# Hybrid decoder layer: small weights laid out by the host, the q block's split pinned behind hT, and the gates' series moved from GpSimd to VectorE

## The chip, the core and the metric

One core of a Trainium2 chip runs the whole layer in one launch. The metric is the device time in microseconds (us) of one execution. The engines are TensorE (PE: matmuls; PEld: its weight loads), VectorE (DVE), ScalarE (ACT), GpSimd (POOL) and SyncE (SP, which issues most DMAs here). Each engine takes its instructions in the order of the program; engines wait for each other by semaphores.

## The reference

The input x has 512 tokens of 1024 channels, all float32. What matters here:

```python
h = rmsnorm(x, norm_mix_g)
proj = h @ w_in
bg, cg, xv, q, k, v, z, a, b, ga, gb = split(proj)
y_a = short_conv_branch(bg, cg, xv, conv_a_w) @ w_a_out
# the gated-DeltaNet branch, 8 heads of 128, chunks of 64
q, k, v = silu(causal_dwconv([q, k, v], gdn_conv_w))   # 4 taps, then l2norm of q and k
beta = sigmoid(b)
g = -exp(A_log) * softplus(a + dt_bias)                # the gates: 512 tokens x 8 heads
G = cumsum(g) in each chunk                            # decays exp(G_i - G_j)
...
x = x + (sigmoid(ga) * y_a + sigmoid(gb) * y_b) @ w_o
x = x + conv_ffn(rmsnorm(x, norm_ffn_g))
out = rmsnorm(x, norm_final_g)
```

softplus(u) is computed as max(u, 0) + log(1 + t) with t = exp(-|u|), and the logarithm by a series: with s = t / (t + 2), log(1 + t) = 2 s (1 + s^2/3 + s^4/5 + ... + s^14/15).

## The kernel before

Matmuls run on pairs of rounded parts: every operand is split into a high part (a cast on ScalarE, `wh` or `hT[0]`) and a rest (a subtraction on VectorE, `wl` or `hT[1]`), and a product is three matmuls. A `Block` is 1 MB of a weight (256 output columns) that is loaded into one of two `raw` buffers and split in four quarters by `part` (L137). `run_jobs` (L204) goes through a list of jobs, one block each: the k block first, then q, v, z of the first pair of heads, and so on. While a job's products are issued, `mm` (L107) counts columns, and at every slab (`SLAB` = 4 matmuls of 512 columns) `tick` (L95) advances the generators in the queues by one step: the next block's split, the evacuations (`qkv` with `conv`, L334: ScalarE scales the product from PSUM to `cv`, VectorE adds the other taps), and the chains. So the number of `yield`s in a chain says how many slabs of matmuls stand in front of its next part in the program. The compiler's scheduler then orders each engine's instructions; `keep_in_program_order` pins single ones, and inside `manual_schedule` the named engines keep the written order.

The start (L427 to L575): SP loads x in four tiles, the small weights and the k block in quarters (`load_k`). `norm_x`, `scale_x` and `turn_x` normalize a tile of x (ScalarE's square sums, VectorE, a power on GpSimd), scale it into `xr` and transpose it on TensorE (L496) into PSUM. `out_hi` (ScalarE, L499) and `out_lo` (VectorE, L503) write the two parts of hT, first for tokens 0 to 255 and then for 256 to 511, times the norm's weight, which lies in `wA`. `round_k` (L507) and `rest_k` (L511) split the k block's quarters. `k_tile` and `ab_tile` are the products of hT with the k block and with the 16 columns of a and b. `wA` holds the conv weights and the norm's, one per partition; they are loaded as rows of 128 (`wr`) and transposed on TensorE (L532), as are `wr2` and `wr3` for `wF` (L573, L574). Three matmuls on zeros (L470, `WARM`) come ahead of all.

The gates (`gates_chain`, L603): the product `abT` of a and b is transposed (L609), `abv` is its sum of parts, `u` is a + dt_bias, `t` = exp(-|u|). The series runs on GpSimd from L624 to L640 and ends in `g`. After `Y_G` = 16 more slabs two matmuls, L644 and L645, form the sums of g in a chunk and over it; G and what follows from it (`negG`, `kdv`, `eG`, `Dm` by way of a DMA) feed the chunks' triangular systems in `front`.

Of the kernel before, what the change touches and what calls it, by code (L numbers as in the profile page):

```python
# [9 lines left out]
F32 = mybir.dt.float32  # L10
F32R = mybir.dt.float32r
AF = mybir.ActivationFunctionType
ALU = mybir.AluOpType
# [3 lines left out]
P = 128  # L17
# [11 lines left out]
Y_V, Y_T, Y_G, Y_N, Y_E, SLAB = 4, 17, 16, 3, 4, 4  # L29
# [31 lines left out]
def layer_kernel(ctx, tc, x, norm_mix_g, w_in, w_ab, conv_a_w, gdn_conv_w, gdn_A_log, gdn_dt_bias,  # L61
                 gdn_norm_g, w_a_out, w_b_out, w_o, norm_ffn_g, w_up, ffn_conv_w, w_down,
# [17 lines left out]
    def bank():  # L80
        return ps.tile([P, 512], F32, tag="ps", name=nm("ps"))
# [43 lines left out]
    class Block:  # L125
        def __init__(self, src, quarter=(4, P)):
            self.src, self.quarter = src, quarter
            self.raw, self.ready, self.lead, self.fed = None, False, 2, True
            self.wh, self.wl = {}, {}
# [7 lines left out]
        def part(self, name, src):  # L137
            wh = self.wh[name] = wp.tile([P, *self.quarter], F32R, tag="wh", bufs=WQ, name=nm("wh"))
            wl = self.wl[name] = wp.tile([P, *self.quarter], F32R, tag="wl", bufs=WQ, name=nm("wl"))
            act.copy(out=wh, in_=src)  # L140
            dve.tensor_tensor(out=wl, in0=src, in1=wh.bitcast(F32), op=ALU.subtract)  # L141
# [206 lines left out]
    pool.memset(phalf, 0.5)  # L348
    wA = const.tile([P, P], F32, name="wA")
    wF = const.tile([P, 133], F32, name="wF")  # L350
# [27 lines left out]
    def load_k(q):  # L378
        nc.sync.dma_start(out=k_block.raw[:, q], in_=w_in[C_K][:, 4 * q:4 * q + 4])
# [47 lines left out]
    with tc.tile_pool(name="st1", bufs=1) as st1:  # L427
# [29 lines left out]
        dtb = gs.tile([P, H], F32, name="dtb")  # L457
        nc.sync.dma_start(out=dtb, in_=gdn_dt_bias[0].partition_broadcast(P))
        alg = gs.tile([P, H], F32, name="alg")
        nc.sync.dma_start(out=alg, in_=gdn_A_log[0].partition_broadcast(P))  # L460
        fr = ffn_conv_w.rearrange("o j (c p) -> (o j c) p", p=P)
        wr2 = st1.tile([66, P], F32, name="wr2")
        nc.sync.dma_start(out=wr2, in_=fr[0:66])
        wr3 = st1.tile([67, P], F32, name="wr3")
        nc.sync.dma_start(out=wr3[0:66], in_=fr[66:132])
        nc.sync.dma_start(out=wr3[66:67], in_=gdn_norm_g)

        po = bank()
        for _ in range(WARM):
            pe.matmul(po[:, 0:512], lhsT=warm[:, 0:P], rhs=warm[:, 0:512], start=True, stop=True)  # L470
        po = bank()
# [21 lines left out]
        def turn_x(t, bs):  # L493
            for k in range(ND):
                c = (k % 2) * HS + (t % 2) * P
                pe.transpose(out=bs[k // 2][:, c:c + P], in_=xrs[t][:, k * P:(k + 1) * P], identity=ident)  # L496
# [31 lines left out]
        with tc.manual_schedule(engines={mybir.EngineType.DVE, mybir.EngineType.Activation, mybir.EngineType.Pool}):  # L528
# [12 lines left out]
            o_ab, o_k = bank(), [bank(), bank()]  # L541
            for ks in (lower, upper):
                for k in ks:
                    out_hi(0, bs, k)
                for k in ks:
                    out_lo(0, bs, k)
                    k_tile(0, k)
                    ab_tile(k)
                if ks is lower:
                    rest_k(1)  # L550
# [21 lines left out]
        po = bank()  # L572
        pe.transpose(out=po[:, 0:66], in_=wr2, identity=ident[:66, :66])  # L573
        pe.transpose(out=po[:, 66:133], in_=wr3, identity=ident[:67, :67])  # L574
        dve.tensor_copy(out=wF, in_=po[:, 0:133])  # L575
# [8 lines left out]
    def hn(ap):  # L584
        return ap.rearrange("p (h n) -> p h n", n=NT)
# [17 lines left out]
    def gates_chain(o):  # L603
# [20 lines left out]
        pool.tensor_scalar(z, t, 2.0, None, op0=ALU.add)  # L624
        yield
        dve.reciprocal(out=beta, in_=beta)
        dve.reciprocal(out=z, in_=z)
        dve.tensor_scalar(u, u, 0.0, None, op0=ALU.max)
# [7 lines left out]
        pool.tensor_tensor(out=q, in0=q, in1=t, op=ALU.mult)  # L636
        pool.tensor_scalar(q, q, 2.0, None, op0=ALU.mult)
        pool.tensor_tensor(out=g, in0=q, in1=u, op=ALU.add)
        pool.tensor_tensor(out=hn(g), in0=hn(g), in1=alg.unsqueeze(2).broadcast_to([P, H, NT]), op=ALU.mult)
        pool.tensor_scalar(g, g, -1.0, None, op0=ALU.mult)  # L640
# [357 lines left out]
    jobs.insert(14, jobs.pop(11))  # L998

# [599 lines left out]
    def down_place(i):  # L1599
# [19 lines left out]
_INS = ['x', 'norm_mix_g', 'w_in', 'w_ab', 'conv_a_w', 'gdn_conv_w', 'gdn_A_log', 'gdn_dt_bias', 'gdn_norm_g',  # L1619
        'w_a_out', 'w_b_out', 'w_o', 'norm_ffn_g', 'w_up', 'ffn_conv_w', 'w_down', 'norm_final_g']  # L1620
# [3 lines left out]
def laid_out(inputs):  # L1624

# [13 lines left out]
    a["w_ab"] = np.ascontiguousarray(w[:, 7168:7184].reshape(ND, P, 16).transpose(1, 0, 2))  # L1639
# [29 lines left out]
```

## Time and profile before

| | |
|---|---|
| median of 3 runs | 966.83 us (965.64 to 966.93) |
| the profiled execution | 966.41 us, span 964.7 us |
| TensorE, VectorE, ScalarE, GpSimd busy | 99%, 77%, 52%, 16% of the span |
| mean granted TensorE clock | 0.996 |
| TensorE busy in 0 to 5, 5 to 10, 10 to 15 us | 3.48, 3.30, 3.51 us |
| TensorE busy in 15 to 20, 20 to 25, 25 to 30 us | 5.00, 4.94, 5.00 us |
| VectorE busy in 30 to 40 us | 9.63 us |

A row of the timeline gives the start in us from the span's start, the duration, the engine, the line of the program, the operation, what it writes and reads, and in brackets how long the engine was idle before it and what ended that. A duration may overlap the next instruction's start, since the engines work in pipelines; so what an instruction costs its queue is the distance from its start to the next one's. A row of waits names the engine and line that waited, what ended the wait, the total in us, how many times, and the longest.

### The profile page before, as it was taken

The page shows a single profiled execution, that of the slowest core. Times are in us where ns is not written, and L with a number is a line of the kernel's source. Part 1 is how long each engine was busy: PE and PEld are TensorE (multiplying, and loading weights), DVE is VectorE, ACT ScalarE, POOL GpSimd, SP SyncE. Part 2 cuts the span into 40 slices and gives each one's busy share as a digit, 9 for nine tenths or more (in the row PEclk, how much of TensorE's full clock was granted, in tenths as well). Part 3 has the DMA queues.
Part 4 walks back from the last instruction along what each step waited for, and adds up shares of the span by engine and source line. Part 5 has one row for each costly group of instructions (what it writes and reads, how often), then busy time and mean ns, then how long its engine had stood idle before and what let it go on. Part 6 is the DMA issues. An engine that isn't in the chain of part 4 may idle for free.

```text
span 964.7 us, 16169 instructions
## 1 busy us (share of the span) xinstructions
PE 951.5 (99%) x6178; PEld 822.6 (85%) x6178; DVE 743.1 (77%) x1401; ACT 505.9 (52%) x1073; POOL 157.1 (16%) x251
## 2 busy tenths in 40 slices
PE   8999999999999999999999999999999999999996
PEld 6888887887878889999988888998889999888885
DVE  5968686796735957799863479999988888969775
ACT  6795656566444424444751235645645456546463
POOL 3330300202000202312232100223222210000000
PEclk9999999999999999999999999999999999999999
DMA  6443422213121456756878436594774783176332
GB/s 227 155 139 95 121 53 89 74 47 103 53 88 45 133 130 138 200 147 160 232 256 173 124 104 225 149 232 154 174 189 177 193 163 131 45 260 230 99 131 87
DMA packets 51630, 138.11 MB, mean 143 GB/s; under 512 B 21692, under 2 KB 22113, under 8 KB 42849
## 3 DMA queue, kind: packets, MB, share of 16 engines
q1 hardware_dynamic: 38864, 107.45, 32.5%
q0 software_dynamic: 12544, 29.37, 16.3%
q8 instruction: 48, 0.79, 0.3%
q14 instruction: 30, 0.24, 0.1%
q10 hardware_dynamic: 144, 0.26, 0.1%
HBM read 133.64 MB, written 32.78 MB: 173 GB/s over the span
## 4 chain that ended last, share of the span: by engine, by line
PE 91%; DVE 4%; ACT 1%; issue 1%; POOL 1%; POOLq 0%
PE ps L108 83%; PE ps L681 1%; PE ps L716 1%; DVE wl L141 1%; PE ps L890 1%; PE ps L910 1%; DVE h L1327 1%; PE ps L899 0%; DVE hn L1313 0%; PE ps L878 0%; PE ps L877 0%; PE ps L854 0%; PE ps L848 0%; POOL r L1311 0%; PE ps L792 0%
## 5 line engine op out<-in xcount | busy, mean ns | idle before, releaser
L108 PE MATMUL ps<-hT,wh 128*128 128x512 f32 (+1 forms) x1104 | 319.1, 368 | 1.6 <-ACT hT L499 1.5
L140 ACT CAST wh<-raw 128x512 fp32r<-128x512 f32 x350 | 203.0, 618 | 220.8 <-PE ps L108 142.5
L141 DVE TENSOR_TENSOR wl<-raw,wh 128x512 fp32r<-128x512 f32 x350 | 232.3, 689 | 58.5 <-ACT wh L140 57.5
L108 PEld LDWEIGHTS ps<-hT,wh 128*128 128x128 f32 x1104 | 197.4, 190 | 30.6 <-ACT hT L499 1.7
L108 PE MATMUL ps<-hT,wl 128*128 128x512 f32 (+1 forms) x552 | 195.4, 362 | 0.0
L108 PE MATMUL ps<-h,wh 128*128 128x512 f32 (+1 forms) x704 | 177.7, 341 | 0.4 <-DVE h L1327 0.4
L108 PEld LDWEIGHTS ps<-h,wh 128*128 128x128 f32 x704 | 122.3, 189 | 15.7 <-DVE h L1327 0.6
L108 PEld LDWEIGHTS ps<-hT,wl 128*128 128x128 f32 x552 | 104.6, 190 | 13.8
L108 PE MATMUL ps<-h,wl 128*128 128x512 f32 (+1 forms) x352 | 114.5, 341 | 0.0
L108 PE MATMUL ps<-wh,xs 128*128 128x512 f32 (+1 forms) x320 | 96.9, 384 | 0.0
L108 PEld LDWEIGHTS ps<-h,wl 128*128 128x128 f32 x352 | 66.6, 189 | 7.6
L108 PEld LDWEIGHTS ps<-wh,xs 128*128 128x128 f32 x320 | 59.6, 188 | 13.1
L223 POOL COPY gate<-raw 1x1 f32<-1x1 f32 x38 | 19.7, 518 | 272.9 <-DMA raw<-in_w_in_dram 119.7
L108 PE MATMUL ps<-wl,xs 128*128 128x512 f32 (+1 forms) x160 | 62.1, 388 | 0.0
L108 PE MATMUL ps<-ts,wh 128*128 128x256 f32 x320 | 56.2, 276 | 0.0
L338 DVE SCALAR_TENSOR_TENSOR cv<-ps,wA,cv 128x511 f32<-128x511 f32 (+2 forms) x72 | 53.2, 741 | 3.9 <-ACT cv L335 3.7
L140 ACT CAST wh<-raws 128x512 fp32r<-128x512 f32 x66 | 39.2, 618 | 26.9 <-PE ps L108 8.6
L141 DVE TENSOR_TENSOR wl<-raws,wh 128x512 fp32r<-128x512 f32 x66 | 42.9, 687 | 12.6 <-ACT wh L140 12.5
L161 DVE TENSOR_TENSOR raw<-raw 128x512 f32<-128x512 f32 x72 | 49.4, 686 | 1.4
L108 PEld LDWEIGHTS ps<-ts,wh 128*128 128x128 f32 x320 | 49.0, 188 | 0.0
L108 PE MATMUL ps<-us,wh 128*128 128x256 f32 x256 | 45.0, 276 | 0.0
L108 PE MATMUL ps<-yas,wh 128*128 128x512 f32 x128 | 40.3, 394 | 0.0
(316 smaller groups left out, 1546.2 us busy)
## 6 DMA issues: line engine op xcount, KB each, us to landing
raw<-in_w_in_dram SPq DMA_DIRECT2D x35, 1024.0 KB, 4.9
raw<-in_w_up_dram SPq DMA_DIRECT2D x22, 1024.0 KB, 5.0
dv<-in_w_down_dram POOLq DMA_DIRECT2D x50, 256.0 KB, 6.2
raws<-dv SPq DMA_DIRECT2D x8, 768.0 KB, 7.2
ov<-in_w_o_dram POOLq DMA_DIRECT2D x20, 256.0 KB, 5.1
raws<-in_w_down_dram SPq DMA_DIRECT2D x10, 512.0 KB, 5.0
raw<-in_w_a_out_dram SPq DMA_DIRECT2D x4, 1024.0 KB, 5.9
raw<-in_w_b_out_dram SPq DMA_DIRECT2D x4, 1024.0 KB, 8.0
```

What stands on the lines that cost most here:

```text
L108: pe.matmul(o, lhsT=a, rhs=b, start=start, stop=stop, skip_group_check=free)
L140: act.copy(out=wh, in_=src)
L141: dve.tensor_tensor(out=wl, in0=src, in1=wh.bitcast(F32), op=ALU.subtract)
L161: dve.tensor_tensor(out=r[q], in0=a, in1=b, op=op)
L223: tc.keep_in_program_order(pool.tensor_copy(out=gate[:, 0:1], in_=el[:, 0:1]))
L338: dve.scalar_tensor_tensor(out=dst[:, sh:], in0=src[:, :S - sh], scalar=wcol(j), in1=dst[:, sh:], op0=ALU.mult, op1=ALU.add)
L681: pe.transpose(out=o[:, n * P:(n + 1) * P], in_=src[:, n * P:(n + 1) * P], identity=ident)
L716: pe.matmul(o[:, i], lhsT=kqs[:, a, h, 0, sl], rhs=kqs[:, b, h, :, sl], start=a > 0, stop=a + b == 0)
L890: pe.matmul(o[:, 0:P], lhsT=TTf[:, f, :], rhs=rs[h], start=True, stop=True)
L910: pe.matmul(o[:, 0:P], lhsT=A[:, f, :], rhs=vns[h], start=True, stop=True)
L1327: dve.tensor_tensor(out=h2[1][:, 4 * g:4 * g + 4, t * P:(t + 1) * P], in0=ov, in1=hs.bitcast(F32), op=ALU.subtract)
```

## The change

- The host lays out the small weights: `small_mix` (what `wA` holds) and `small_rest` (what `wF` holds, with A_log and dt_bias repeated over the partitions) come by one DMA each, already with one value per partition. The transposes and copies from `wr`, `wr2` and `wr3` are gone. SP issues the first quarter of the k block ahead of the small weights.
- TensorE gets five matmuls of 128 columns on zeros (`busy`), three after the first tile's transposes and two after the second's, and is named in `manual_schedule`.
- In the first products `rest_k` stands behind two `out_lo`, and the products with `wl` come after those with both parts of hT (`first_tiles`).
- The second job's block (q) is `pinned`: its casts and rests keep their place in the program, behind hT.
- The gates' series runs on VectorE, and its sums come after 8 slabs instead of 16 (`Y_G`).

```diff
-Y_V, Y_T, Y_G, Y_N, Y_E, SLAB = 4, 17, 16, 3, 4, 4
+Y_V, Y_T, Y_G, Y_N, Y_E, SLAB = 4, 17, 8, 3, 4, 4
...
-            act.copy(out=wh, in_=src)
-            dve.tensor_tensor(out=wl, in0=src, in1=wh.bitcast(F32), op=ALU.subtract)
+            ops = act.copy(out=wh, in_=src), dve.tensor_tensor(out=wl, in0=src, in1=wh.bitcast(F32), op=ALU.subtract)
+            if self.pinned:
+                for op in ops:
+                    tc.keep_in_program_order(op)
...
         load_x(0)
         load_x(1)
-        wr = st1.tile([P, P], F32, name="wr")
-        nc.sync.dma_start(out=wr[0:96], in_=gdn_conv_w.rearrange("o j (c p) -> (o j c) p", p=P))
-        nc.sync.dma_start(out=wr[96:120], in_=conv_a_w.rearrange("o j (c p) -> (o j c) p", p=P))
-        nc.sync.dma_start(out=wr[120:128], in_=norm_mix_g.rearrange("o (c p) -> (o c) p", p=P))
+        load_k(0)
+        nc.sync.dma_start(out=wA, in_=small_mix)
         ab_raw = st1.tile([P, ND, 16], F32, name="ab_raw")
-        nc.sync.dma_start(out=ab_raw, in_=w_ab)
-        load_k(0)
+        nc.sync.dma_start(out=ab_raw, in_=small_ab)
         load_k(1)
...
+        nc.sync.dma_start(out=rest_w, in_=small_rest)
...
+        def first_tiles(ks, q):
+            for i, k in enumerate(ks):
+                out_lo(0, bs, k)
+                if i == 1:
+                    rest_k(q)
+                for e in (0, 1):
+                    mm(o_k[0][:, 0:HS], piece(k_block.wh, 0, k), hT[e][:, k, 0:HS], k == 0 and e == 0, False)
+                ab_tile(k)
+            for k in ks:
+                mm(o_k[0][:, 0:HS], piece(k_block.wl, 0, k), hT[0][:, k, 0:HS], False, k == ND - 1)
...
             turn_x(0, bs)
-            pe.transpose(out=po[:, 0:P], in_=wr, identity=ident)
+            busy(3, P)
             norm_x(1)
             round_k(0)
-            dve.tensor_copy(out=wA, in_=po[:, 0:P])
             scale_x(1)
             turn_x(1, bs)
+            busy(2, P)
             ab_split()
             round_k(1)
-            rest_k(0)
...
         pool.tensor_scalar(beta, beta, 1.0, None, op0=ALU.add)
-        pool.tensor_scalar(z, t, 2.0, None, op0=ALU.add)
+        dve.tensor_scalar(z, t, 2.0, None, op0=ALU.add)
+        dve.reciprocal(out=z, in_=z)
+        dve.tensor_tensor(out=t, in0=t, in1=z, op=ALU.mult)
+        dve.tensor_tensor(out=z, in0=t, in1=t, op=ALU.mult)
+        dve.tensor_scalar(q, z, 1.0 / 15.0, None, op0=ALU.mult)
+        for c in (13, 11, 9, 7, 5, 3):
+            dve.scalar_tensor_tensor(out=q, in0=q, scalar=1.0 / c, in1=z, op0=ALU.add, op1=ALU.mult)
+        dve.scalar_tensor_tensor(out=q, in0=q, scalar=1.0, in1=t, op0=ALU.add, op1=ALU.mult)
+        dve.tensor_scalar(u, u, 0.0, None, op0=ALU.max)
+        dve.scalar_tensor_tensor(out=g, in0=q, scalar=2.0, in1=u, op0=ALU.mult, op1=ALU.add)
+        dve.scalar_tensor_tensor(out=hn(g), in0=hn(g), scalar=-1.0, in1=alg.unsqueeze(2).broadcast_to([P, H, NT]),
+                                 op0=ALU.mult, op1=ALU.mult)
         yield
         dve.reciprocal(out=beta, in_=beta)
-        dve.reciprocal(out=z, in_=z)
-        dve.tensor_scalar(u, u, 0.0, None, op0=ALU.max)
-        yield
-        pool.tensor_tensor(out=t, in0=t, in1=z, op=ALU.mult)
-        pool.tensor_tensor(out=z, in0=t, in1=t, op=ALU.mult)
-        pool.tensor_scalar(q, z, 1.0 / 15.0, 1.0 / 13.0, op0=ALU.mult, op1=ALU.add)
-        for c in (11, 9, 7, 5, 3, 1):
-            pool.tensor_tensor(out=q, in0=q, in1=z, op=ALU.mult)
-            pool.tensor_scalar(q, q, 1.0 / c, None, op0=ALU.add)
...
+    jobs[1][0].pinned = True
```

What the scheduler makes of it, at three places. First TensorE, where the gates' sums stand. Before: `ps_620` is the first product of the third job (v) and `g_456` the gates.

```order
L108 MATMUL ps_585<-hT_81,wh_463 128x512 x2
L108 MATMUL ps_585<-hT_81,wh_432 128x512 x2
L108 MATMUL ps_620<-hT_82,wh_545 128x512
L108 MATMUL ps_620<-hT_81,wl_546 128x512
...
L108 MATMUL ps_620<-hT_82,wh_545 128x512
L108 MATMUL ps_620<-hT_81,wl_546 128x512
L644 MATMUL ps_647<-g_456,triu 128x32
L645 MATMUL ps_647<-g_456,ones 128x32
L108 MATMUL ps_620<-hT_82,wh_555 128x512
```

The change: `ps_515` is the q block's first product (24 matmuls), `ps_577` its second.

```order
L107 MATMUL ps_515<-hT_82,wh_405 128x512
L107 MATMUL ps_515<-hT_81,wl_406 128x512
L107 MATMUL ps_515<-hT_81,wh_393 128x512 x2
L107 MATMUL ps_515<-hT_81,wh_405 128x512 x2
L107 MATMUL ps_515<-hT_81,wh_393 128x512 x2
L107 MATMUL ps_515<-hT_81,wh_405 128x512 x2
L640 MATMUL ps_564<-g_443,triu 128x32
L641 MATMUL ps_564<-g_443,ones 128x32
L107 MATMUL ps_577<-hT_82,wh_450 128x512
```

The sums have moved from the v block's first product to the place right behind the q block's first, 36 matmuls of 512 columns earlier.

Then VectorE between the taps of k's first product and those of q's first. Before, `cv_488` and `cv_541` are k's two products, `wl` are rests of q's and v's blocks:

```order
L338 SCALAR_TENSOR_TENSOR cv_488<-ps_204,wA,cv_488 128x511
L627 RECIPROCAL z_454<-z_454 128x32
L628 TENSOR_SCALAR u_452<-u_452 128x32
L338 SCALAR_TENSOR_TENSOR cv_488<-ps_204,wA,cv_488 128x510
L338 SCALAR_TENSOR_TENSOR cv_541<-ps_205,wA,cv_541 128x511
L338 SCALAR_TENSOR_TENSOR cv_488<-ps_204,wA,cv_488 128x509
L338 SCALAR_TENSOR_TENSOR cv_541<-ps_205,wA,cv_541 128x510
L141 TENSOR_TENSOR wl_566<-raw_396,wh_565 128x512
```

The change, the last rows of the series; `kqs` are the rests of k's conv output and `cv_592` is the q block's first product `ps_515`:

```order
L339 SCALAR_TENSOR_TENSOR cv_520<-ps_194,wA,cv_520 128x509
L629 SCALAR_TENSOR_TENSOR q_442<-q_442,z_441 128x32
L139 TENSOR_TENSOR wl_545<-raw_383,wh_544 128x512
L629 SCALAR_TENSOR_TENSOR q_442<-q_442,z_441 128x32
L139 TENSOR_TENSOR wl_553<-raw_383,wh_552 128x512
L629 SCALAR_TENSOR_TENSOR q_442<-q_442,z_441 128x32
L139 TENSOR_TENSOR wl_632<-raw_513,wh_631 128x512
L630 SCALAR_TENSOR_TENSOR q_442<-q_442,t_440 128x32
L966 TENSOR_TENSOR kqs_501<-kq_500,kqs_501 128x512
L632 SCALAR_TENSOR_TENSOR g_443<-q_442,u_439 128x32
L339 SCALAR_TENSOR_TENSOR cv_592<-ps_515,wA,cv_592 128x511
L633 SCALAR_TENSOR_TENSOR g_443<-g_443,rest_w 128x32
```

Each operation of the series now has a wide one in front of it, 15 from the first tap of `cv_487` (k's first product) on, and the last operation on g stands behind a tap of the q block's first product.

Last VectorE in the first products. Before, `wl_201` and `wl_234` are the rests of k's first two quarters and `hT_82` is hT's second part:

```order
L392 TENSOR_TENSOR ab_114<-ab_raw,ab_114 128x8x16
L513 TENSOR_TENSOR wl_201<-raw_102,wh_183 128x512
L503 SCALAR_TENSOR_TENSOR hT_82<-ps_153,wA,hT_81 128x256 x2
L503 SCALAR_TENSOR_TENSOR hT_82<-ps_154,wA,hT_81 128x256 x2
L513 TENSOR_TENSOR wl_234<-raw_102,wh_199 128x512
```

The change, where `wl_205` and `wl_235` are the same rests:

```order
L396 TENSOR_TENSOR ab_114<-ab_raw,ab_114 128x8x16
L499 SCALAR_TENSOR_TENSOR hT_82<-ps_141,wA,hT_81 128x256 x2
L509 TENSOR_TENSOR wl_205<-raw_102,wh_173 128x512
L499 SCALAR_TENSOR_TENSOR hT_82<-ps_142,wA,hT_81 128x256 x2
L499 SCALAR_TENSOR_TENSOR hT_82<-ps_143,wA,hT_81 128x256 x2
L509 TENSOR_TENSOR wl_235<-raw_102,wh_190 128x512
```

The first rest has moved from ahead of hT's second part to behind its first two tiles.

More of the change, by code (lines that the diff above doesn't have):

```diff
@@ L127, in __init__ @@
             self.src, self.quarter = src, quarter
-            self.raw, self.ready, self.lead, self.fed = None, False, 2, True
+            self.raw, self.ready, self.lead, self.fed, self.pinned = None, False, 2, True, False
             self.wh, self.wl = {}, {}
@@ L349, in layer_kernel @@
     wA = const.tile([P, P], F32, name="wA")
-    wF = const.tile([P, 133], F32, name="wF")
+    rest_w = const.tile([P, 133 + 2 * H], F32, name="rest_w")
+    wF = rest_w[:, 0:133]
+    dtb, alg = rest_w[:, 133:133 + H], rest_w[:, 133 + H:133 + 2 * H]
     room = {}
@@ L456, in layer_kernel, with busy @@
         load_k(2)
[L457 to L466, printed above, removed]
+        nc.sync.dma_start(out=rest_w, in_=small_rest)
         po = bank()
-        for _ in range(WARM):
-            pe.matmul(po[:, 0:512], lhsT=warm[:, 0:P], rhs=warm[:, 0:512], start=True, stop=True)
-        po = bank()
+        def busy(n, cols):
+            for _ in range(n):
+                pe.matmul(po[:, 0:cols], lhsT=warm[:, 0:P], rhs=warm[:, 0:cols], start=True, stop=True)
+        busy(WARM, S)
         sst = st1.tile([P, 2 * NT], F32, name="sst")
@@ L527, in layer_kernel @@
         k_block.ready = True
-        with tc.manual_schedule(engines={mybir.EngineType.DVE, mybir.EngineType.Activation, mybir.EngineType.Pool}):
+        with tc.manual_schedule(engines={mybir.EngineType.DVE, mybir.EngineType.Activation, mybir.EngineType.Pool,
+                                         mybir.EngineType.PE}):
             norm_x(0)
@@ L571, in layer_kernel @@
                     out_lo(HS, bs, k)
[L572 to L575, printed above, removed]
     gdn_w = lambda c: (lambda j: wA[:, j * 24 + c:j * 24 + c + 1])
@@ L1638, in laid_out @@
     a["w_in"] = cols(np.concatenate([w[:, :7168], w[:, 7184:]], axis=1))
-    a["w_ab"] = np.ascontiguousarray(w[:, 7168:7184].reshape(ND, P, 16).transpose(1, 0, 2))
+    a["small_ab"] = np.ascontiguousarray(w[:, 7168:7184].reshape(ND, P, 16).transpose(1, 0, 2))
+    groups = lambda *names: [a[n].reshape(-1, P).T for n in names]
+    heads = [np.broadcast_to(a[n].reshape(1, -1), (P, a[n].size)) for n in ("gdn_dt_bias", "gdn_A_log")]
+    a["small_mix"] = np.concatenate([*groups("gdn_conv_w", "conv_a_w", "norm_mix_g")], axis=1)
+    a["small_rest"] = np.concatenate([*groups("ffn_conv_w", "gdn_norm_g"), *heads], axis=1)
     for n in ("w_a_out", "w_b_out", "w_up"):
```

21 lines of the change are left out of this document (5 added, 16 removed).

## The prediction

> **What bounds the kernel now.** I read the page first (its busy shares and its chain of work that ended last), then the list of TensorE's waits, then the timeline of the two places that the change touches: the first 24 us, and the gates around 27 to 45 us.
>
> ```profile
> span 964.7 us, 16169 instructions
> PE 951.5 (99%) x6178; PEld 822.6 (85%) x6178; DVE 743.1 (77%) x1401; ACT 505.9 (52%) x1073; POOL 157.1 (16%) x251
> ...
> PE 91%; DVE 4%; ACT 1%; issue 1%; POOL 1%; POOLq 0%
> ```
>
> TensorE is busy for 99% of the span and carries 91% of the chain. So nothing counts but TensorE's work and TensorE's waits. All its waits, by who ended them (us in total, times, longest):
>
> ```profile
> PE ps L496 <- DVE xr L491: 1.6, 2, 1.2
> PE ps L470 <- DVE warm L431: 1.5, 1, 1.5
> PE ps L108 <- ACT hT L499: 1.5, 1, 1.5
> PE ps L681 <- DVE vs L929: 0.5, 1, 0.5
> PE ps L108 <- DVE h L1327: 0.4, 1, 0.4
> PE ps L108 <- DVE hT L503: 0.2, 1, 0.2
> ```
>
> They come to 5.7 us, and all but 0.9 of it (L681, L1327) is the start, before hT is there. L644 and L645, the gates' sums, are not on the list: today they wait for nothing. So the change can win something at the start alone, and it can lose wherever it makes TensorE wait. The sum is made against the profiled run's own 966.41 us, which is 0.42 under the median of 966.83.
>
> **Step 1, the start: worth 0.6 us.** Four windows of TensorE (busy us, clock granted, DMA share, GB/s), then ScalarE, VectorE and TensorE on the way to the second half of hT:
>
> ```profile
> 4.86:8.27 3.41, 2.35 (x12) 1.00 0.76 245
> 8.27:11.69 3.42, 1.45 (x11) 1.00 0.86 304
> 11.69:15.10 3.41, 3.25 (x16) 0.50 0.70 230
> ```
>
> ```profile
> 9.57 0.62 ACT L509 CAST wh<-raw 128x512 fp32r<-128x512 f32 x1 [2.19 <-DMA raw<-in_w_in_dram]
> 10.10 0.29 ACT L391 CAST ab<-ab_raw 128x128 fp32r<-128x128 f32 x1
> 10.29 0.61 ACT L509 CAST wh<-raw 128x512 fp32r<-128x512 f32 x1
> 10.81 3.02 ACT L499 ACTIVATE hT<-ps,wA 128x256 fp32r<-128x256 f32 x8
> ...
> 13.25 0.68 DVE L513 TENSOR_TENSOR wl<-raw,wh 128x512 fp32r<-128x512 f32 x1
> 13.85 1.65 DVE L503 SCALAR_TENSOR_TENSOR hT<-ps,wA,hT 128x256 fp32r<-128x256 f32 x4
> 18.46 0.75 DVE L491 TENSOR_SCALAR xr<-xt,rt 128x1024 f32<-128x1024 f32 x1 [0.44 <-POOL rt L486]
> ...
> 19.40 1.91 PE L496 MATMUL ps<-ident,xr 128*128 128x128 f32 x16
> 20.69 0.47 ACT L499 ACTIVATE hT<-ps,wA 128x256 fp32r<-128x256 f32 x1 [3.75 <-PE ps L496]
> ```
>
> Today the clock is halved for 3.4 us from 11.69 on, behind a stretch with 1.45 us of work in 3.42. TensorE is therefore late: the last scaled x is ready at 18.46 + 0.75 = 19.21, but its eight transposes are the second half of the sixteen from 19.40, about 20.3, and the second hT waits for them at 20.69. The change acts in three ways.
>
> The first quarter of k is now issued ahead of the small weights, so its cast and that of ab (0.62 and 0.29) no longer stand between its landing and the second quarter's cast at 10.29. The bytes ahead of that second quarter are the same, so it lands no sooner than they allow: somewhere between 9.57 and 10.29. That is 0 to 0.7 us; I take 0.2, nearest to the equal bytes.
>
> VectorE's rest of k's first quarter, done today while hT is awaited, moves behind the first two hT parts. Its step from start to start is 13.85 - 13.25 = 0.60, so the last scaled x comes at 19.21 + 0.60 - 0.20 = 19.6. That is still ahead of today's 20.3.
>
> The five new matmuls of 128 columns lie in TensorE's waits of 1.2 us (L491) and 1.5 us (L499). Priced as two transposes each (1.91 / 16 = 0.12) they take 0.7 and 0.5 us, so they cost nothing. They raise the work in the 8.27 stretch from 1.45 to about 2.0 of 3.42. That lies between 1.45, behind which the clock fell, and 2.35, behind which it held. If it holds, TensorE is ready in time and the last transposes start at 19.65 instead of 20.3: a gain of 0.6, which I take. If it falls as today, the gain is 0; a loss is excluded, since 19.6 is ahead of 20.3. If the second quarter of k lands at 9.57 as well, the gain is 0.65 + 0.5 + 0.1, about 1.3 us. So 0 to 1.3.
>
> The removed transposes of the small weights and VectorE's copies of them are 0.1 to 0.3 us each in stretches where their engine waits: nothing. SP issues fewer transfers and the q block sooner; its products begin at 31.36 (row below), so that is nothing either. Its casts and rests, now held behind hT in program order, end around 30: the fourth is used last, at 36.8.
>
> **Step 2, the gates' series: a wait of 3.7 us.** Today GpSimd runs it, first and last row, and TensorE comes for it late:
>
> ```profile
> 30.50 0.29 POOL L624 TENSOR_SCALAR z<-t 128x32 f32<-128x32 f32 x1 [0.78 <-ACT t L621]
> ...
> 41.09 0.29 POOL L640 TENSOR_SCALAR g<-g 128x32 f32<-128x32 f32 x1
> ...
> 31.36 0.40 PE L108 MATMUL ps<-hT,wl 128*128 128x512 f32 x1
> 36.82 0.39 PE L108 MATMUL ps<-hT,wl 128*128 128x512 f32 x1
> ...
> 44.76 0.30 PE L644 MATMUL ps<-g,triu 128*128 128x32 f32 x2
> ```
>
> g is there at 41.38, the sums are at 44.76: 3.4 us of slack. In the new order the sums stand right behind the q block's first 24 products. Those start today at 31.36, and the 25th is the row at 36.82. So on today's clock TensorE reaches the sums at 36.8. Both this and VectorE's side hang on the second hT, so step 1 shifts both alike.
>
> VectorE's side: its series does not run in one piece. The order shows it threaded through 15 wide operations that stand between its first tap and the last operation on g. Rows of today for what stands there:
>
> ```profile
> 27.30 0.23 DVE L612 COPY abv<-ps 128x64 f32<-128x64 f32 x1 [0.50 <-PE ps L609]
> 27.44 0.68 DVE L141 TENSOR_TENSOR wl<-raw,wh 128x512 fp32r<-128x512 f32 x1
> 28.04 0.21 DVE L613 TENSOR_TENSOR abv<-abv,ps 128x64 f32<-128x64 f32 x1
> 28.77 0.18 DVE L616 TENSOR_TENSOR u<-abv,dtb 128x32 f32<-128x32 f32 x1
> 28.87 0.68 DVE L141 TENSOR_TENSOR wl<-raw,wh 128x512 fp32r<-128x512 f32 x1
> 30.83 0.35 DVE L627 RECIPROCAL z<-z 128x32 f32<-128x32 f32 x1
> 31.10 0.12 DVE L628 TENSOR_SCALAR u<-u 128x32 f32<-128x32 f32 x1
> 37.98 0.74 DVE L338 SCALAR_TENSOR_TENSOR cv<-ps,wA,cv 128x511 f32<-128x511 f32 x1
> 38.64 0.68 DVE L141 TENSOR_TENSOR wl<-raw,wh 128x512 fp32r<-128x512 f32 x1
> ...
> 28.45 0.69 ACT L335 ACTIVATE cv<-ps,wA 128x512 f32<-128x512 f32 x1
> 37.14 0.68 ACT L335 ACTIVATE cv<-ps,wA 128x512 f32<-128x512 f32 x1
> ```
>
> The first tap waits for ScalarE's scaling, 28.45 + 0.69 = 29.1, so 29.2. Then from start to start: 7 taps at 38.64 - 37.98 = 0.66, and 8 splits (six wl, two kqs) at 28.04 - 27.44 = 0.60, together 9.4. Of the series 14 operations stand behind that tap: a reciprocal at 31.10 - 30.83 = 0.27, and 13 that no row shows in this place. Their bounds are 0.10 (u, 28.87 - 28.77) and the 0.18 that u lasts; I take 0.12, since each one's input was finished one wide operation earlier: 1.6. So g is ready at 29.2 + 9.4 + 0.3 + 1.6 = 40.5, and TensorE, which has come at 36.8, waits 3.7 us. Behind it on TensorE stands everything else; nothing there can pass it.
>
> Bounds: the slow end takes 0.18 for each and 0.5 us of waits on ScalarE, whose casts feed the splits: 41.8, a wait of 5. The fast end is fixed by the order, whatever VectorE's speed. The tap on the q block's first product stands ahead of the last operation on g, and that product ends just before TensorE comes to the sums. Today ScalarE scales it at 37.14 and VectorE taps it from 37.98 to 38.72; with the last operation g is there at 38.9, so a wait of 2.1 at least.
>
> GpSimd's 21 removed operations ran beside a busy TensorE: no gain. G, its transpose and Dm come sooner than today; no wait on the list is theirs, so nothing again.
>
> **Step 3, the clock behind that wait: 1.5 us.** The windows above say it: 3.42 - 1.45 = 2.0 us without work in one stretch of 3.4 us brought 3.4 us at half clock, 1.06 us (the 4.86 stretch) did not. A wait of 3.7 us leaves at least 1.85 us in one of the two stretches that it touches, and mostly over 2. So I expect one stretch at half clock: 16 matmuls in 11.69 to 15.10 against 31 in the next, so half of 3.4 us, 1.7, less what of it falls into the wait itself: 1.5. Bounds 0 and 2.2.
>
> The Trainium skill ("TensorE: Matmul & The Clock Gate", "HAM oscillation") puts the rule at no idle gaps over about 3.4 us, and its Part 1 lets the clock drop after an idle window. By that rule a wait of 3.7 us would hardly ever hold a whole idle window, and the sum would be 969.5. This trace differs: its clock fell behind a stretch that was 42% busy, so I go by the row.
>
> **The sum.** 966.41 - 0.6 + 3.7 + 1.5 = 971.0 us, 0.43% over the median. About 0.2% (1.9 us) is what a measurement of this kernel can tell from no change.
>
> **The rivals.**
> The clock holds behind the wait: 966.41 - 0.6 + 3.7 = 969.5. For it speaks that a wait may split evenly over two stretches; against it the 1.45 row.
>
> The wait is short, at its floor: 966.41 - 0.9 + 2.1 = 967.6, up to 968.6 with 2.8. It needs VectorE to be 1 to 1.6 us ahead of my sum, and a wait that short leaves the clock alone.
>
> The series is in time. Its operations cost VectorE less than GpSimd's, and if g were there by 36.8, TensorE would wait for nothing: 966.41 - 0.6 = 965.8. It would have to be 3.7 us earlier, and the tap on the q block's product speaks against it. The Trainium skill ("GPSIMD Engine Reference", 4.1 "Engine selection") sends elementwise work to VectorE, GpSimd being about twice as slow: half of the 10.9 us from 30.50 to 41.38 would end at 35.9, in time, and give this rival's 965.8. It leaves out what else stands in VectorE's queue.
>
> The other side, not slower: the start gives more than the sums take. If both quarters of k landed by 8.7, hT could follow the second transposes from about 9.3 instead of 10.81, and with the clock held the start would gain up to 2.1. With the wait at its floor that is 966.4. It decides where the start's gain passes the wait; the equal bytes ahead of the second quarter speak against it.
>
> **How the numbers follow.** Forecast 0.50; clock holds 0.23; short wait 0.15; series in time 0.06; start outweighs 0.06. The first two are slower by over 0.2% (0.73, and 0.02 of the third); the third and most of the last two lie within 0.2%; faster keeps 0.05, for the two last with the start at its best. The range is 967.2 (start 1.3, wait 2.1, clock held) to 972.8 (start 0.3, wait 4.6, clock 2.1); what lies outside is the two last rivals and little above.
>
> **What would show it.** Right: TensorE's waits list L640 behind VectorE's g (L633), one time, some 3 to 4 us, near 36; the granted clock falls to 0.50 for one stretch within 4 us of it; the windows at 8 to 15 us show a full clock and the second hT starts near 20.0. Wrong: no row for L640, or a wait under 2.1, or the clock at 1.00 after it. The weakest term is the 13 small operations' 0.12, then the clock.

## The result and the profile after

The changed kernel takes 977.13 us (median of 4: 976.60 to 978.28); the kernel before, run beside it, 966.24. The ratio is 1.0119, with a 95% interval of 1.0107 to 1.0131: 1.2% slower. The forecast was 971.0 with a range from 967.2 to 972.8: the direction was right, some 6 us were missing.

TensorE's busy time and its list of waits after:

```profile
span 974.9 us, 16161 instructions
...
PE 961.1 (99%) x6185; PEld 829.7 (85%) x6185; DVE 744.2 (76%) x1412; ACT 505.6 (52%) x1071; POOL 146.7 (15%) x230
```

```profile
PE ps L640 <- DVE g L633: 3.8, 1, 3.8
PE ps L465 <- DVE warm L435: 1.5, 1, 1.5
PE ps L107 <- DVE hT L499: 0.7, 2, 0.5
PE ps L677 <- DVE vs L925: 0.5, 1, 0.5
PE ps L107 <- ACT hT L495: 0.3, 1, 0.3
PE ps L107 <- DVE h L1324: 0.2, 1, 0.2
```

The predicted wait is there, 3.8 us for 3.7. But the list now adds up to 7.0 us, against 5.7 before: 1.3 more, while the span is 10.2 longer. The rest stands in the first fence: TensorE's busy time went from 951.5 to 961.1, though the change gives it no new products. Part of that is the clock. Its windows (start:end, us, busy us and count, granted clock, DMA share, GB/s) from ahead of the wait until after it:

```profile
30.25:33.66 3.41, 3.41 (x16) 1.00 0.73 281
33.66:37.07 3.41, 1.30 (x6) 1.00 0.00 0
37.07:40.48 3.41, 1.74 (x6) 0.50 0.89 305
40.48:43.89 3.41, 3.41 (x10) 0.50 0.04 12
43.89:47.30 3.41, 3.41 (x17) 1.00 0.92 308
```

The wait (34.96 to 38.74) touches two stretches, with 1.30 and 1.74 us of work in 3.41, and each is followed by one at half clock. The other part is spread over hundreds of microseconds and sits in no wait. It shows in the groups of matmuls, kept apart by shape; the last columns are busy us and the mean ns of one. Before, and then after:

```profile
L108 PE MATMUL ps<-h,wh 128*128 128x256 f32 x320 | 60.7, 284 | 0.4 <-DVE h L1327 0.4
L108 PE MATMUL ps<-ts,wh 128*128 128x256 f32 x320 | 56.2, 276 | 0.0
L108 PE MATMUL ps<-us,wh 128*128 128x256 f32 x256 | 45.0, 276 | 0.0
L108 PE MATMUL ps<-wh,xs 128*128 128x512 f32 x304 | 94.1, 390 | 0.0
```

```profile
L107 PE MATMUL ps<-h,wh 128*128 128x256 f32 x320 | 60.8, 284 | 0.2 <-DVE h L1324 0.2
L107 PE MATMUL ps<-ts,wh 128*128 128x256 f32 x320 | 58.6, 282 | 0.0
L107 PE MATMUL ps<-us,wh 128*128 128x256 f32 x256 | 46.9, 282 | 0.0
L107 PE MATMUL ps<-wh,xs 128*128 128x512 f32 x304 | 95.5, 395 | 0.0
```

`h,wh` is as it was; `ts,wh`, `us,wh` and `wh,xs` are 5 to 6 ns longer each, from 358 us on, where the change touches nothing. One stretch of 20 us with `ts`, its matmuls alone, before and after, at full clock:

```profile
425.00:445.00 20.00, 11.24 (x96) 1.00 0.58 146
```

```profile
432.00:452.00 20.00, 11.72 (x96) 1.00 0.61 154
```

Each stretch has 96 of them, and after the change they take 0.48 us more, 5 ns each. From start to start in the trace, the mean of `ts,wh` goes from 113.6 to 118.8 ns. Summed over all matmuls with `ts` and `us` (864) that is 4.4 us, over those with `xs` 1.7 and with `mix` 0.4: 6.4 us. (With `yas` it cancels: `yas,wh` is 2.0 ns slower, `yas,wl` 4.2 faster.) The first of the two fences of groups tells more: in the kernel before, two groups of one shape, 128 x 256, differ by 8 ns (`h,wh` 284, `ts,wh` 276). So the shape alone does not set the pace; it also matters which two tiles meet.

What these tiles have in common is where they lie. The change puts `dtb` and `alg` behind `wF` in `rest_w`, so the constants' pool grows by 16 floats, 64 bytes per partition, and the gates' pool loses them. In the compiled program all that is allocated between the two, `wh` and `wl`, `hT`, `h`, `yb`, moves up by 64 bytes (the first `wh` from 19232 to 19296, hT from 68384 to 68448), while `ts` (135136), `us` and `xs` (151520), `yas` and `mix`, which are allocated from the other end, stay. `hT,wh` and `h,wh` moved together; `ts,wh`, `us,wh`, `wh,xs` did not.

### The profile page after: what moved, and what is told of

Its sections match the earlier page's. It is cut to its first block, busy times and chain, and to the rows that moved or that the text cites. A ratio compares the mean times of both kernels' runs of the same rounds, so it can differ in the third digit from the quotient of the medians.

```text
span 974.9 us, 16161 instructions
## 1 busy us (share of the span) xinstructions
PE 961.1 (99%) x6185; PEld 829.7 (85%) x6185; DVE 744.2 (76%) x1412; ACT 505.6 (52%) x1071; POOL 146.7 (15%) x230
## 4 chain that ended last, share of the span: by engine, by line
PE 90%; DVE 5%; ACT 1%; issue 1%; POOL 1%; DMA 1%; SPq 0%; POOLq 0%; ACTq 0%
PE ps L107 83%; PE ps L677 1%; DVE wl L139 1%; PE ps L712 1%; PE ps L886 1%; PE ps L906 1%; DVE cv L339 1%; DMA raw<-in_w_in_dram 1%; DVE h L1324 0%; PE ps L895 0%; DVE hn L1310 0%; PE ps L874 0%; PE ps L873 0%; PE ps L850 0%; PE ps L844 0%
## 5 line engine op out<-in xcount | busy, mean ns | idle before, releaser
L139 DVE TENSOR_TENSOR wl<-raw,wh 128x512 fp32r<-128x512 f32 x350 | 232.3, 687 | 62.8 <-ACT wh L139 61.8
L224 POOL COPY gate<-raw 1x1 f32<-1x1 f32 x38 | 16.4, 431 | 281.2 <-DMA raw<-in_w_in_dram 121.1
L107 PE MATMUL ps<-ts,wh 128*128 128x256 f32 x320 | 58.6, 282 | 0.0
```

Source lines behind the costliest of these rows:

```text
L107: pe.matmul(o, lhsT=a, rhs=b, start=start, stop=stop, skip_group_check=free)
L139: ops = act.copy(out=wh, in_=src), dve.tensor_tensor(out=wl, in0=src, in1=wh.bitcast(F32), op=ALU.subtract)
L224: tc.keep_in_program_order(pool.tensor_copy(out=gate[:, 0:1], in_=el[:, 0:1]))
```

## The experiments

Names in a pair are the moving operand, then the stationary one. "Distance" is the address of the stationary tile less that of the moving one, modulo 256 bytes: `ts,wh` has 64 before and 128 after, `wh,xs` 192 and 128, `yas,wh` 64 and 128, `hT,wh` 0 in both.

**The places alone, in the kernel before.**

```diff
-        dtb = gs.tile([P, H], F32, name="dtb")
+        dtb = const.tile([P, H], F32, name="dtb")
...
-        alg = gs.tile([P, H], F32, name="alg")
+        alg = const.tile([P, H], F32, name="alg")
```

> The kernel before, with one thing changed: the two small tiles dtb and alg (32 bytes per partition each) come from the constants' pool and not from the gates' pool, so that the weight pieces wh and wl, hT and h lie 64 bytes higher, as in the changed kernel, while ts, us, yas, xs and mix stay where they were. Theory (placement): a matmul whose two operands come one from each side steps slower: ts,wh and us,wh from 113.6 to 118.8 ns, wh,xs from 222 to 227 ns; sum over their counts some 6 us, so 972 us. Rival (the slower steps come from what runs beside them in the changed kernel, or from the clock): no change, 966.2 us, and 113.6 ns.

Measured: 971.73 us against 965.38, ratio 1.0061 (1.0048 to 1.0074). No instruction is added, removed or moved, and the kernel is 0.6% slower; `ts,wh` again steps at 118.8 ns, and `wh,xs` with 512 columns at 232.2 instead of 227.5 (the expectation's 222 and 227 are means with 15 matmuls of 256 columns among them). Summed over the groups as above that is 6.4 us. Its groups:

```profile
L108 PE MATMUL ps<-wh,xs 128*128 128x512 f32 x304 | 95.5, 395 | 0.0
...
L108 PE MATMUL ps<-ts,wh 128*128 128x256 f32 x320 | 58.6, 282 | 0.0
```

**The changed kernel at the old places.**

```diff
-    rest_w = const.tile([P, 133 + 2 * H], F32, name="rest_w")
-    wF = rest_w[:, 0:133]
-    dtb, alg = rest_w[:, 133:133 + H], rest_w[:, 133 + H:133 + 2 * H]
+    wF = const.tile([P, 133], F32, name="wF")
...
-        nc.sync.dma_start(out=rest_w, in_=small_rest)
+        heads = gs.tile([P, 2 * H], F32, name="heads")
+        dtb, alg = heads[:, 0:H], heads[:, H:2 * H]
+        nc.sync.dma_start(out=wF, in_=small_rest[:, 0:133])
+        nc.sync.dma_start(out=heads, in_=small_rest[:, 133:133 + 2 * H])
```

> The changed kernel with the small weights loaded into two tiles (133 columns in the constants' pool, 16 in the gates' pool), so that every tile from the weight pool on lies where it lay before. Theory (placement): ts,wh steps at 113.6 ns again, the wait at the gates' sums (3.8 us) and the half clock behind it stay; 977.1 - 6 = 971 us. Rival: 977 us, the steps at 118.8 ns.

Measured: 971.21 us, ratio 1.0063 (1.0050 to 1.0076) to the kernel before, and `ts,wh` at 113.7 ns again. That is 5.9 us less than the changed kernel by the medians; by the two ratios to the kernel before (1.0119 and 1.0063), which was 966.24 in one set of runs and 965.38 in the other, it is 5.4. With the places taken out, the change costs 5.8 us over the kernel before; the forecast was 4.6 over its base.

**The sums behind 16 slabs again**, first in the changed kernel, then also at the old places.

```diff
-Y_V, Y_T, Y_G, Y_N, Y_E, SLAB = 4, 17, 8, 3, 4, 4
+Y_V, Y_T, Y_G, Y_N, Y_E, SLAB = 4, 17, 16, 3, 4, 4
```

> The changed kernel with Y_G = 16, so that the gates' sums stand 16 slabs behind the series as before. Theory: the wait of 3.8 us and both stretches at half clock (some 2.4 us) go, the slower steps stay: 977.1 - 6.2 = 970.9 us. Rival (the half clock of 37 to 44 us has another cause than the wait): 977.1 - 3.8 = 973.3 us. Rival (the wait goes on to another place): 975 us or more.

> The changed kernel with both: sums behind 16 slabs, and every tile from the weight pool on where it lay before. Theory: only the start's gain is left, some 1.9 us (TensorE came to the place of the gates' sums at 34.96 and not at 36.82): 964.3 us, faster than the kernel before by 0.2%. Rival (the start's gain is given back later): 966.2 us.

Measured: 971.62 us (1.0065, 1.0053 to 1.0078) and 965.93 us (1.0005, 0.9996 to 1.0014). In the first, the wait and the half clock behind it are gone, 5.5 us together by the medians and 5.2 by the ratios; the slow steps stay. In the second both are gone, and what is left, the start and the series on VectorE, is worth nothing: the second expectation's theory failed, its rival holds. Its profiled execution shows why the one good start in the profile after was no measure. TensorE's waits in it begin with:

```profile
PE ps L107 <- ACT hT L496: 1.9, 1, 1.9
```

**The gates' series alone, in the kernel before** (the changed kernel's 15 operations, 14 of them behind the first tap, and `Y_G = 8`; old start, old places).

> The kernel before with the gates' series of the changed kernel alone (14 operations on VectorE, sums behind 8 slabs); its start, its small weights and all places in SBUF stay. Theory: the wait at the sums for VectorE's g and the half clock behind it, the same as in the changed kernel, since both sides hang on the second hT: +5.3, so 970.7 us. Rival (in the changed kernel the wait is long because TensorE is sooner there): a wait of about 2 us and +2 to +3, 968 us.

Measured: 972.02 us against 965.96, ratio 1.0059 (1.0041 to 1.0077), so +5.7 (4.0 to 7.4). The wait is as long with the old start:

```profile
PE ps L641 <- DVE g L634: 3.9, 1, 3.9
```

**Pairs of operands by themselves.** Groups of 16 matmuls, the stationary tile's four pieces and the moving tile's pieces in turn, each group with its own offset:

```python
for r in range(16): pe.matmul(o[:, 0:512], lhsT=sta[:, 16 + 128 * (r % 4):144 + 128 * (r % 4)],
                              rhs=mov[:, 512 * (r % 2):512 + 512 * (r % 2)], start=r == 0, stop=r == 15)  # distance 64
```

> No layer is computed: only groups of 16 matmuls in float32r, 128 x 256 (and at the end 128 x 512), with no other engine at work; each group has its own distance between the address of the moving tile and that of the stationary one, in steps of 32 bytes, and some groups move both together. Theory (the pace hangs on the distance of the two operands in SBUF alone): pace differs between the groups by some 5 ns (113 to 119 ns for 256 columns), it repeats with a period, and groups in which both are moved by the same amount agree. Rival (the two operands matter only together with what other engines read or write at the same time): all groups alike within 1 ns. Rival (the address of one operand alone decides): groups with equal distance differ when both are moved.

Groups of 512 columns, one line of the program each: L168 has distance 0, L172 64, L176 128, L180 192, L184 256 and L200 512 bytes.

```profile
L172 PE MATMUL o<-mov,sta 128*128 128x512 f32 x16 | 3.9, 396 | 0.0
...
L176 PE MATMUL o<-mov,sta 128*128 128x512 f32 x16 | 3.9, 394 | 0.0
...
L180 PE MATMUL o<-mov,sta 128*128 128x512 f32 x16 | 3.8, 392 | 0.0
...
L168 PE MATMUL o<-mov,sta 128*128 128x512 f32 x16 | 3.8, 391 | 0.0
...
L184 PE MATMUL o<-mov,sta 128*128 128x512 f32 x16 | 3.8, 390 | 0.0
...
L200 PE MATMUL o<-mov,sta 128*128 128x512 f32 x16 | 3.8, 389 | 0.0
```

From start to start the means at 0, 64, 128, 192, 256 and 512 bytes are 228.5, 233.5, 232.3, 229.5, 226.7 and 226.7 ns (at 0 the first five steps are slower, the rest 226 or 227). With TensorE alone on the core, distance sets the pace: up to 7 ns in 227, the same again at 256 more (320: 233.5, 384: 232.4, 448: 229.5). For 256 columns the means lie between 116.7 and 120.1 ns, with the same period, and groups with equal distance agree within 0.2 ns where both tiles are moved by 64 bytes (0: 119.5 and 119.3; 64: 117.9 and 117.9; 128: 118.7 and 118.7). So no other engine is needed for it. Moves of both by 32 or 96 bytes do change it (distance 96: 117.3, then 120.0 and 118.8), so distance is not all: within 64 bytes the address has a part of its own, which the kernel's moves by whole 64 bytes leave alone. One thing the groups do not give: the 113.6 ns of `ts,wh` at distance 64, where they have 117.9. The slower 118.8 after the change is theirs. So for `ts` and `us`, which carry 4.4 of the 6.4 us, only the kernels show the effect, not the groups. A difference that was not tried: in the compiled programs the kernel's tiles lie 32 bytes past a multiple of 64, while in the groups whose distance is a multiple of 64 both tiles lie on one.

**Larger moves.** Small tiles of the gates' pool go to the constants' pool, in the kernel before:

```diff
-    small = lambda n: gs.tile([P, 32], F32, name=n)
+    small = lambda n: (const if n in ('beta', 'negG') else gs).tile([P, 32], F32, name=n)
```

> The kernel before with two of the gates' small tiles (beta and negG, 128 bytes each) taken from the constants' pool, so that the weight pieces, hT and h lie 256 bytes higher and ts, us, yas, xs, mix stay. Theory (the pace hangs on the distance of the two operands modulo 256 bytes): all distances are those of the kernel before again, 965.9 us, ts,wh at 113.6 ns, although the move is four times that which cost 6 us. Rival (any move away from the places of before costs): 971 us or more.

> As the last, with beta alone: 128 bytes. Theory: by the groups of matmuls run by themselves, the distance of wh from ts goes from 64 to 192 (117.9 and 117.8 ns there, so no change), that of xs from wh from 192 to 64 (229.5 and 233.5 ns, 456 matmuls, +1.8 us), that of wh from yas from 64 to 192 (-0.7 us), so 967 us. Rival (the cost grows with the size of the move): 978 us. Rival (ts is fast only at the one distance of 64): 971 us.

Measured: 256 bytes 965.89 us (0.9999, 0.9990 to 1.0008), 128 bytes 971.26 us (1.0051, 1.0036 to 1.0065). The period is 256 bytes in the kernel too: a move four times as large as the harmful one costs nothing. At 128 bytes the groups by themselves led to 967, and the kernel took the rival's 971: `ts,wh` steps at 118.0 there, so of the distances 64, 128 and 192 only 64 is fast for it. `xs` did what the groups say (`wh,xs` with 512 columns at 233.3 ns at distance 64, the groups 233.5).

**Putting the distance to use.** `xs`, `yas` and `mix` are moved by 64 bytes, so that `wh,xs`, `wh,mix` and `yas,wh` come to distance 0, and `ts,wh` keeps 64:

```diff
+    def shifted(pool_, tag, name, by, shape):
+        t = pool_.tile([P, ND * S + 64], F32R, tag=tag, name=name)[:, by:by + ND * S]
...
-            st["xs"] = [st["up"].tile([P, 4, 4, HS], F32R, tag=f"t{e}", name=f"xs{e}") for e in range(2)]
+            st["xs"] = [shifted(st["up"], f"t{e}", f"xs{e}", 16, (4, 4, HS)) for e in range(2)]
```

(`yas` and `mix` alike with 16 floats, `ts` and `us` with 0.)

> The kernel before with xs, yas and mix each 64 bytes higher within tiles that are 256 bytes longer; ts, us and all else keep their places modulo 256 bytes. Theory: 64 bytes more bring the distance of xs and mix from the weight pieces, and of the weight pieces from yas, to 0 modulo 256, where 128 x 512 ran at 226.7 ns; yas from 233.3 (192 of them, -1.3 us), wl,xs from 231 (152, -0.7), mix from 231 (132, -0.6): 963.3 us, faster than before by 0.27%. Rival (the pace in the kernel is set by more than this distance): no change or slower.

> The changed kernel with sums behind 16 slabs, before's places, and xs, yas and mix 64 bytes higher within longer tiles (the last alone took the kernel before from 965.75 to 962.66 us). Theory (the three are independent, the start and the series on VectorE are worth nothing): 965.9 - 3.1 = 962.8 us, the same as the kernel before with the tiles moved. Rival (the start is worth 0.6 us or more, hidden so far by scatter): 962 us or less.

Measured: 962.66 us in the kernel before (0.9967, 0.9955 to 0.9979) and 962.85 in the changed one with late sums and old places (0.9972, 0.9962 to 0.9983). Both beat both kernels; the first, whose instructions are those of the kernel before, is the simplest. The groups moved as the pairs say; in the kernel before with the tiles moved:

```profile
L108 PE MATMUL ps<-wl,xs 128*128 128x512 f32 x152 | 59.2, 389 | 0.0
...
L108 PE MATMUL ps<-yas,wh 128*128 128x512 f32 x128 | 39.6, 389 | 0.0
```

Before they were at 394 each. From start to start `yas,wh` went from 233.3 to 226.8 ns, `wl,xs` with 512 columns from 231.7 to 226.0. Over all groups the steps explain 2.7 of the 3.1 us.

**The start without its five small matmuls** (late sums, old places).

```diff
-            busy(3, P)
...
-            busy(2, P)
```

> The changed kernel with sums behind 16 slabs and before's places (which took 965.9 us), without the five small matmuls that keep TensorE at work among the first transposes. Theory (they hold the clock at the start in some executions): the windows behind 8 us show more stretches at half clock and the time is 0.5 to 1.5 us more, 967 us. Rival (when k's second quarter lands decides it): 965.9 us, no change.

Measured: 967.15 us (1.0010, 1.0000 to 1.0020). The median is what the theory put, but its worth is not shown: the same kernel with the five took 965.93 in another set (1.0005, 0.9996 to 1.0014), and the two intervals overlap. Four windows of this kernel, all engines' busy us and counts, then the clock, DMA share and GB/s:

```profile
8.30:11.70 3.40, 1.50 (x9) 1.12 (x9) 0.80 (x4) 1.74 (x6) 0.00 (x0) 0.95 1.02 397
11.70:15.10 3.40, 3.08 (x14) 2.64 (x14) 3.40 (x8) 3.40 (x9) 0.00 (x0) 0.50 0.93 369
15.10:18.50 3.40, 3.40 (x20) 3.15 (x18) 2.96 (x8) 1.79 (x4) 1.36 (x2) 0.55 0.02 10
18.50:22.00 3.50, 3.50 (x33) 3.48 (x31) 0.84 (x2) 0.00 (x0) 3.03 (x11) 1.00 0.71 215
```

Behind 1.50 us of work in 3.40 the clock is halved for nearly 7 us (0.95, 0.50 and 0.55 in three windows).

**The sums behind 12 slabs** (changed kernel, old places, `Y_G = 12`).

> The changed kernel at before's places with the sums behind 12 slabs (8 took 971.2 us, 16 took 965.9). A slab is four products of 512 columns, 4 x 0.227 = 0.91 us, so four more slabs are 3.6 us of other work ahead of the sums. Theory (the wait is only the order: g comes when it comes): of the wait of 3.8 us 0.2 are left, no half clock behind it, 966 us. Rival (VectorE's series slides along with TensorE's products, whose taps stand in front of it): a wait of 2 us or more is left, and 968 to 970 us.

Measured: 971.38 us (1.0064, 1.0050 to 1.0078), no better than 8. The theory was right on the wait named, and wrong on the time: the wait at the sums is gone, and one as long stands 22 us later. The rival's 968 to 970 was missed too.

```profile
PE ps L107 <- DVE kn L699: 3.9, 1, 3.9
```

ScalarE's part of it (the squares that kn's PSUM tile waits for are L698, the decays' exponentials L598):

```profile
53.23 1.28 ACT L598 ACT_TABLE_LOAD   x1
54.52 0.40 ACT L598 ACTIVATE Dm<-Dm,negG 128x128 f32<-128x128 f32 x1
54.83 0.60 ACT L966 CAST kqs<-kq 128x512 fp32r<-128x512 f32 x1
55.34 2.16 ACT L598 ACTIVATE Dm<-Dm,negG 128x128 f32<-128x128 f32 x7
57.40 0.26 ACT L698 ACTIVATE junk<-ps 128x128 f32<-128x128 f32 x1
57.55 0.20 ACT L698 ACTIVATION_READ_ACCUMULATOR junk<-ps 128x1 f32 x1
57.77 1.28 ACT L962 ACT_TABLE_LOAD   x1
```

With sums four slabs sooner the decays come ready sooner, and their exponentials, with a table load on either side, fall among the squares of the second half of k; 16 slabs put them behind the last square (L598 begins at 54.98 there, after eight), and 8 slabs ahead of the first (52.79, the first square at 56.97). This is read from one trace of each; no run moves the exponentials alone. By it, `Y_G` sets not only when g must be there but where the whole chain behind it meets ScalarE's queue.

## Why the prediction was wrong where it was, step by step

**What bounds the kernel.** The step that failed is the sentence "nothing counts but TensorE's work and TensorE's waits", read as if the work were fixed. The work was priced as unchanged, and by the steps it grew by 6.4 us without one product more. A move of 64 bytes is shown as the cause from both sides: put into the kernel before it costs 0.61%, taken out of the changed one it gives back 0.56%, 5.4 to 5.9 us. The term was missing from the sum, and from the rivals; the tile `rest_w`, which is larger than `wF`, and the two rows of equal shape (284 and 276 ns) were there to be read. The signs that the prediction named for being right nearly all came: L640 behind L633 with 3.8 us (at 34.96, for "near 36"), half clock within 4 us, full clock from 8 to 15 us, the second hT at 19.03. None of them looks at the pace of the matmuls, so they could not tell that the time was wrong.

**Step 2, the wait: 3.7 us, measured 3.8** (3.9 in the kernel with the gates alone). Its parts hold too: from the first tap at 27.44 to g at 38.59 it is 11.2 us, where 11.3 were summed. Of the 13 small operations 11 start 0.09 or 0.10 us ahead of the next wide one and two 0.17 or 0.18, in the mean 0.11, where 0.12 was taken. The last of them:

```profile
36.16 0.18 DVE L629 SCALAR_TENSOR_TENSOR q<-q,z 128x32 f32<-128x32 f32 x1
36.26 0.68 DVE L139 TENSOR_TENSOR wl<-raw,wh 128x512 fp32r<-128x512 f32 x1
36.86 0.18 DVE L630 SCALAR_TENSOR_TENSOR q<-q,t 128x32 f32<-128x32 f32 x1
37.04 0.69 DVE L966 TENSOR_TENSOR kqs<-kq,kqs 128x512 fp32r<-128x512 f32 x1
37.65 0.18 DVE L632 SCALAR_TENSOR_TENSOR g<-q,u 128x32 f32<-128x32 f32 x1
37.75 0.74 DVE L339 SCALAR_TENSOR_TENSOR cv<-ps,wA,cv 128x511 f32<-128x511 f32 x1
38.41 0.18 DVE L633 SCALAR_TENSOR_TENSOR g<-g,rest_w 128x32 f32<-128x32 f32 x1
```

The tap at 37.75 ahead of the last operation is the one on which the floor of 2.1 us rested. The rival by which VectorE, twice as fast, would be in time ("GPSIMD Engine Reference", 4.1, of the Trainium skill) fell by just this queue. That section gives the factor of about two for operations with two inputs, which 11 of the 21 removed ones have, so the estimate of 35.9 also used it too widely.

**Step 3, the clock: 1.5 us, from one stretch; it was two.** Both stretches that the wait touches had under 1.8 us of work in 3.41, and both were followed by half clock. The rival in which the clock holds had its sign wrong: the wait did split nearly evenly, and that left too little work on both sides. Of the ten products of 512 columns behind the wait that ran at half clock, most start 0.43 us apart instead of 0.23; together they lost 2.2 us, and the four small matmuls of the sums 0.5 more. Wait and clock together were put at 5.2; taking them out gave 5.5 and 5.3 us by the medians. One stretch, as forecast, is what the wait of the run with 12 slabs brought. The Trainium skill ("TensorE: Matmul & The Clock Gate", HAM oscillation: no idle gap over about 3.4 us) warns of a wait of 3.8 us; the prediction read it together with Part 1 of that page, by which the clock drops after a whole idle window, and so found it nearly free. In the trace neither stretch was idle throughout, and the clock was halved for 6.8 us, so the row of 1.45 was the better guide.

**Step 1, the start: -0.6 us forecast, nothing measured** (965.93 to 965.38, interval -0.04% to +0.14%). In the profile after, the clock held through the start and TensorE came to the sums at 34.96 instead of 36.82, more than forecast. That was one execution. Over the runs, the place where the sum went wrong is k's second quarter, which was bounded "somewhere between 9.57 and 10.29": ScalarE's second cast begins at 8.97 us in the profile after and at 10.65 in the same start with late sums and old places.

```profile
8.97 0.62 ACT L505 CAST wh<-raw 128x512 fp32r<-128x512 f32 x1 [0.81 <-DMA raw<-in_w_in_dram]
```

```profile
10.65 0.62 ACT L506 CAST wh<-raw 128x512 fp32r<-128x512 f32 x1 [2.58 <-DMA raw<-in_w_in_dram]
```

So the landing moves by 1.7 us between executions. In the six traces with the changed start and its five small matmuls, the clock held in the four where this cast began by 9.82, and fell in the two where it began at 10.65 and 10.96; with the old start it fell in all six. The base, too, was one execution with half clock at the start (964.7 us span) where the kernel before, over 17 runs, has spans from 962.4 to 965.1. So in some executions the start gains, as far as TensorE's arrival at the sums shows it; why no median shows it is left open.

**The sum.** Of its three terms the wait is exact (3.8 for 3.7), the clock is about 0.7 us or more short in the trace and 0.1 to 0.3 short with the wait by the runs, the start, at +0.5 (-0.4 to +1.4) for -0.6, is about 1 us too good, and a fourth term of about 6 us is missing. The kernel that has the three without the fourth, at the old places, took 971.21. That this is so near the forecast's 971.0 is partly luck: it stands over a kernel before of 965.38, the forecast over 966.41.

## What to carry to other kernels

Where a change alters the size of any tile, look up which tiles it moves against which: compare the groups of matmuls by tile pair, shape by shape, before and after, and let a group that the change does not touch but that has a new mean be the first lead. Before a forecast, rows of one shape with different means can be a warning that the pace hangs on placement, and point to a gain that a few bytes of padding bring. A reader moved forward by a few slabs should be followed past its own wait, to where the work behind it lands in the queues of the other engines; and a start that waits on DMA should be read from several executions, not from one profile.

## What the runs showed of the hardware

- The pace of back-to-back float32r matmuls hangs on the distance in SBUF between the moving and the stationary operand, modulo 256 bytes, for moves by whole 64 bytes: 226.7 ns at 256 and 512, and 233.5 at 64 and 320, for 512 columns; in the kernel 113.6 ns at 64 and 118.8 at 128 for 256 columns. The Trainium skill ("SBUF — State Buffer", "SBUF: two separate sides") lets only the port pair that VectorE and GpSimd share contend on the engines' side; here TensorE, alone on the core, is up to 7 ns slower by the places of its own two operands. Whether its weight loads and its moving reads meet in a bank was not tried, nor why `ts,wh` in the kernel steps faster at 64 than the pairs by themselves.
- The clock changed in steps of 3.41 us. Counted in such stretches, in all 12 traces with a half clock it fell behind every stretch with at most 1.73 us of work, and held behind every one with at least 2.09. Once halved, it stayed so behind stretches with 1.74, 2.83, 2.86 and 3.09 us of work, and rose behind 3.08 and behind 3.24 or more. So the wait at the sums cost two stretches (6.8 us) in three traces, even in two of them where it lay almost within one (0.1 and 0.2 us of work in it), and the wait in the run with 12 slabs cost one (3.4 us).
- With the five small matmuls in the start, some executions took more around the span: 1.7 to 2.9 us between a run's time and its span, where all 12 runs of the kernel without them, and the 17 of the kernel before beside the first experiments, have 1.7 to 1.8. The cause is open.
